# Gate/up products of a hybrid encoder layer: one 512-wide matmul for two 256-wide ones, five PSUM banks per unit, and 21 weight pieces summed during w_out

## The chip, the cores and the metric

One NeuronCore of a Trainium2 chip runs the kernel. The time is device microseconds (us) of one execution. TensorE (PE in the profile) multiplies and accumulates in PSUM, eight banks of 128 x 512 fp32; VectorE (DVE), ScalarE (ACT) and GpSimd (POOL) work beside it, and SyncE (SP) starts most DMAs. Each engine runs its own instructions in order; semaphores tie them together.

## The reference

One encoder layer on 512 tokens of width 2048, all fp32:

```python
h = rmsnorm(x, attn_norm_w)
... # projection w_in, windowed attention, gated linear attention -> concatenated heads
x = x + concat @ w_out
h = rmsnorm(x, ffn_norm_w)
x = x + (silu(h @ w_gate) * (h @ w_up)) @ w_down      # hidden width 5632
return rmsnorm(x, final_norm_w)
```

The change is in h @ w_gate and h @ w_up, each 512 x 2048 times 2048 x 5632.

## The kernel before

**fp32 as two parts.** TensorE takes a rounded fp32 format here. So every operand is split: a rounded part, "hi", cast by ScalarE, and the remainder, "lo" (value minus hi), made by VectorE. A product is three matmuls: hi x hi, hi x lo and lo x hi.

**Buffers.** SBUF work space is two sets of slots, s2 (70 of 128 x 512; "a" in the profile) and s4 (16 of 128 x 1024; "b"). PSUM banks are slots too ("ps"). A slot that is put back goes to the end of its queue of free ones; the next instruction that writes it waits for its last reader.

**Order.** All instructions are written out in one program order. Stages up to w_out are jobs (`run_job`, L268 to L316): each goes through its weights in halves, three matmuls (L304 to L306) per bank and k tile, with weights loaded by SP (512 KB, at most three held) and split up to `AHEAD` = 3 halves ahead. After each half `run_side` takes steps from two lists of generators, `urgent` first. The w_out stage is jobs 12 to 15, one per 512 output columns, 16 halves each; at each job's end VectorE adds the result to x (L1062), POOL loads the next part of x (`load_res`), and `urgent` work squares, stores (xd), transposes and builds the gate/up operands (`pair_operands`, L1028).

**Gate/up (class `Feed`, L1181 to L1283).** Each product of 2 x 2 blocks is done in seven block products instead of eight, at the price of sums before and after (the scheme of Strassen and Winograd). A block of weights is 128 x 128, a block of x is 128 x 256 (half the tokens). There are 44 units: 22 blocks of 256 columns, the gate's and then the up's. A unit goes through the depth of 2048 in 4 pieces; a piece has two pairs of k tiles (p = 0, 1). So there are 176 pieces of 2 x 7 x 3 = 42 matmuls, all 256 wide (L1216 to L1218). Per piece:

- SP loads 512 KB of weights into an s4 slot (L1136), up to three pieces ahead.
- VectorE makes four sums of weight blocks in another slot with three additions (L1157 to L1159), two pieces ahead.
- ScalarE casts three raw blocks (768 columns) and the four sums (1024) to hi (L1170); VectorE makes the remainders (L1175), one piece ahead.
- PE does the products into four banks; two products share a bank.

On the side of x, `pair_operands` makes seven blocks for each pair of k tiles (`xs[q]`, q = 0 to 7): B11, B21, B22 and the sums T1 to T4, each as hi and lo. B11 lies with hi and lo side by side in one slot; the others lie two to a slot, with hi in one slot and lo in another.

After a unit's last piece, `evac` (L1222 to L1246) joins the products in steps, one taken by `run_urgent` in each later piece: ScalarE copies 256 columns out of PSUM (L1232), VectorE adds and subtracts (L1227, the helper's line, and L1235) into an s4 slot. `finish` then scales and applies silu to a gate block (L1253, L1254), or multiplies an up block with the gate's (L1257) and has POOL store it (L1259) for the w_down stage. The first step falls one piece after the unit's end.

`run` (L1262) orders each piece: new banks, loads, split of this piece if still open, sums of the next two, split of the next, products, an urgent step.

Of the kernel before, what the change touches and what calls it, by code (L numbers as in the profile page):

```python
# [23 lines left out]
P = 128  # L24
# [87 lines left out]
def put(*slots):  # L112
    for s in slots:
        if s.home is not None:
            s.home.free.append(s.i)


def layer(nc, tc, x, attn_norm_w, w_in, rel_table, gw_f, gb_f, gw_b, gb_b, gla_norm_w, w_out,
# [7 lines left out]
    with tc.manual_schedule(), \  # L126
# [27 lines left out]
        state = {"credit": 0.0, "set": None}  # L154


        class Stream:
# [93 lines left out]
        class Job:  # L251
            drop = None
            between = None
            tail = None
            banks = None

        def job(kind, pieces, kts, acts, evac, rate=0.0, before=None, start=None, limit=None):

# [9 lines left out]
        def run_job(j):  # L268
# [6 lines left out]
            for i in range(j.n):  # L275
# [754 lines left out]
        def pair_operands(q, fs_):  # L1030

            a, z = slice(0, 256), slice(256, 512)
            f1, f2 = fs_
            t13, t24 = s2.get(), s2.get()
            sub = lambda o, x_, y_: dve.tensor_tensor(o, x_, y_, op=OP.subtract)
            sub(t13.t[:, a], f1.t[:, a], f1.t[:, z])
            sub(t13.t[:, z], f2.t[:, z], f1.t[:, z])
            dve.tensor_tensor(t24.t[:, a], f2.t[:, z], t13.t[:, a], op=OP.add)
            sub(t24.t[:, z], t24.t[:, a], f2.t[:, a])
            yield  # L1040
            todo = []
            slots = []
            for src, n in ((f1.t[:, a], 256), (f2.t, 512), (t13.t, 512), (t24.t, 512)):
                sl, hi, lo, hf = half_split(src, n)
                slots += sl
                todo.append((src, hi, lo, hf))
            for i in range(4):
                src, hi, lo, hf = todo[i]
                act.copy(hi, src)
                sub(lo, src, hf)  # L1050
                put((f1, f2, t13, t24)[i])
                if i % 2:
                    yield
            (_, b1h, b1l, _), (_, f2h, f2l, _), (_, t13h, t13l, _), (_, t24h, t24l, _) = todo
            xs[q] = dict(slots=slots, B11=(b1h, b1l), B21=(f2h[:, a], f2l[:, a]), B22=(f2h[:, z], f2l[:, z]),
                         T1=(t13h[:, a], t13l[:, a]), T3=(t13h[:, z], t13l[:, z]),
                         T2=(t24h[:, a], t24l[:, a]), T4=(t24h[:, z], t24l[:, z]))

        def evac_out(c):
            def f(banks):  # L1060
# [60 lines left out]
        class Blocks:  # L1121
# [9 lines left out]

            def load(self):
                while self.n_load < self.n and len(self.raw) < self.most and s4.free:
                    w, k, n_kt, col, n = self.source(*self.seq[self.n_load])
                    r = s4.get(F32, self.shape(4))
                    sp.dma_start(out=r.t.rearrange("p a b c -> p (a b c)").rearrange("p (k c) -> p k c", k=n_kt),  # L1136
                                 in_=w[k * P:(k + n_kt) * P, col:col + n].rearrange("(k p) c -> p k c", p=P))
                    self.raw[self.n_load] = r
                    self.n_load += 1

            def sums(self, i, halves=False):

# [38 lines left out]
        class Feed(Blocks):  # L1181

            def __init__(self):
                self.units = [(w, j) for j in range(FF // 256) for w in (w_gate, w_up)]
                self.per = NP // 2
                seq = [(u, q) for u in range(len(self.units)) for q in range(self.per)]
                seq.insert(self.per + 1, seq.pop(self.per - 1))  # L1190
                self.begin(seq, 2, P)

            def source(self, u, q):
                w, j = self.units[u]
                return w, 4 * q, 4, j * 256, 256

            def products(self, i, banks):
                st_ = self.sets.pop(i)
                piece = self.seq[i][1]
                first, last = piece == 0, piece == self.per - 1  # L1200
                a, z = slice(0, 256), slice(256, 512)
                A, B, C, E = (b.t for b in banks)
                for p in range(2):
                    q = 2 * piece + p
                    (rh, rl), (sh, sl) = st_
                    R = lambda n: (rh.t[:, p, n], rl.t[:, p, n])
                    Z = lambda n: (sh.t[:, p, n], sl.t[:, p, n])
                    x_ = xs[q]
                    prods = [(A[:, a], R(0), x_["B11"], True), (A[:, z], R(2), x_["B21"], False),
                             (B[:, a], Z(2), x_["T2"], True), (C[:, a], Z(1), x_["T1"], True),  # L1210
                             (C[:, z], Z(0), x_["T3"], False), (E[:, a], Z(3), x_["B22"], True),
                             (E[:, z], R(1), x_["T4"], False)]
                    for o, (wh, wl), (xh, xl), head in prods:
                        head = head and first and p == 0
                        end = last and p == 1
                        mm(o, wh, xh, start=head, stop=False, skip_group_check=True)  # L1216
                        mm(o, wh, xl, start=False, stop=False, skip_group_check=True)  # L1217
                        mm(o, wl, xh, start=False, stop=end, skip_group_check=True)  # L1218
                for hi, lo in st_:
                    put(hi, lo)  # L1220

            def evac(self, u, banks):  # L1222


                a, z = slice(0, 256), slice(256, 512)
                w, j = self.units[u]
                add = lambda o, x_, y_: dve.tensor_tensor(o, x_, y_, op=OP.add)  # L1227
# [4 lines left out]
                act.copy(t1.t[:, a], A[:, a])  # L1232
                add(c[:, a], A[:, z], t1.t[:, a])
                put(banks[0])
                dve.tensor_tensor(t1.t[:, z], t1.t[:, a], B[:, a], op=OP.subtract)  # L1235
                yield
# [7 lines left out]
                put(banks[1])  # L1244
                self.finish(u, c_, c)
                yield  # L1246

            def finish(self, u, c_, c):
                w, j = self.units[u]
                if w is w_gate:  # L1250
                    tables(SILU)
                    for f in range(2):
                        dve.tensor_tensor(c_.t[:, f], c_.t[:, f], rb[2 + f].t, op=OP.mult)  # L1253
                    act.activation(c_.t, c_.t, AF.Silu)  # L1254
                    self.gate = c_
                else:
                    dve.tensor_tensor(c_.t, c_.t, self.gate.t, op=OP.mult)  # L1257
                    put(self.gate)
                    pool.dma_start(out=gd[j], in_=c)  # L1259
                    put(c_)  # L1260

            def run(self):  # L1262
                banks = {}
                for i, (u, q) in enumerate(self.seq):
                    if u not in banks:
                        banks[u] = [ps.get() for _ in range(4)]
                    self.most = 5 if i < 2 else 3
                    self.load()
                    self.split(i)
# [2 lines left out]
                    self.split(i + 1)  # L1272
                    if i < 2:
                        self.sums(self.n_sums, halves=True)
                    self.products(i, banks[u])
                    if u == len(self.units) - 1:
                        for p in (2 * q, 2 * q + 1):
                            put(*xs.pop(p)["slots"])
                        down_start(q)
                    for _ in range(3 if i < 2 else 2 if i < 8 else 1):  # L1280
                        run_urgent()
                    if q == self.per - 1:
                        urgent.append(self.evac(u, banks.pop(u)))  # L1283

        ff = Feed()

# [417 lines left out]
            return run  # L1704

        run_last = finish()
        for n, j in enumerate(jobs):
            if n == n_down:
                dn.run()
# [2 lines left out]
                load_wf()  # L1712
            run_job(j)
            if n == n_out:
                ff.run()
        drain()
        run_last()
# [27 lines left out]
```

## Time and profile before

| | us |
|---|---|
| three runs | 2215.52, 2215.56, 2216.87 |
| median | 2215.56 |
| profiled execution | 2216.53 |
| its span, first to last instruction | 2214.8 |
| w_out stage on PE | about 688 to 863 |
| gate/up stage on PE | 862.8 to 1752.4 |

The profile is of one execution. Its page gives the busy time of each engine, the span in slices, the queues, the chain of work that ended last and the costliest groups of instructions. Further views ask the same trace: groups of a window, waits of one engine with what ended them, instructions in order of time, and tables of windows. The granted TensorE clock was 0.999 of full speed.

### The profile page before, as it was taken

The page shows a single profiled execution, that of the slowest core. Times are in us where ns is not written, and L with a number is a line of the kernel's source. Part 1 is how long each engine was busy: PE and PEld are TensorE (multiplying, and loading weights), DVE is VectorE, ACT ScalarE, POOL GpSimd, SP SyncE. Part 2 cuts the span into 40 slices and gives each one's busy share as a digit, 9 for nine tenths or more (in the row PEclk, how much of TensorE's full clock was granted, in tenths as well). Part 3 has the DMA queues.
Part 4 walks back from the last instruction along what each step waited for, and adds up shares of the span by engine and source line. Part 5 has one row for each costly group of instructions (what it writes and reads, how often), then busy time and mean ns, then how long its engine had stood idle before and what let it go on. Part 6 is the DMA issues. An engine that isn't in the chain of part 4 may idle for free.

```text
span 2214.8 us, 37040 instructions
## 1 busy us (share of the span) xinstructions
PE 2204.3 (100%) x14842; PEld 2040.1 (92%) x14842; DVE 1623.5 (73%) x2740; ACT 1003.0 (45%) x1664; POOL 96.0 (4%) x149
## 2 busy tenths in 40 slices
PE   9999999999999999999999999999999999999998
PEld 7888888888888888999999999999999999999987
DVE  4366665745454438988888888888888888888795
ACT  5244444444444345444434343444343465565462
POOL 0000000000000100000000000000000010011300
PEclk9999999999999999999999999999999999999999
DMA  6525625231324332334334333343333775575982
GB/s 207 162 82 158 169 87 141 76 124 57 96 67 153 131 127 77 115 115 124 115 115 124 115 124 115 115 125 115 115 125 115 249 164 179 167 195 143 288 316 76
DMA packets 210185, 302.26 MB, mean 136 GB/s; under 512 B 15005, under 2 KB 133197, under 8 KB 210014
## 3 DMA queue, kind: packets, MB, share of 16 engines
q1 hardware_dynamic: 194366, 258.87, 37.3%
q0 software_dynamic: 15328, 40.51, 7.2%
q8 instruction: 116, 1.90, 0.4%
q10 hardware_dynamic: 320, 0.53, 0.1%
q14 instruction: 55, 0.45, 0.1%
HBM read 246.58 MB, written 40.70 MB: 130 GB/s over the span
## 4 chain that ended last, share of the span: by engine, by line
PE 99%; DVE 1%; DMA 0%; SPq 0%; ACT 0%; issue 0%; DVEq 0%
PE ps L1217 13%; PE ps L1216 13%; PE ps L1218 13%; PE ps L304 7%; PE ps L306 7%; PE ps L305 7%; PE ps L297 5%; PE ps L295 5%; PE ps L296 5%; PE ps L1457 5%; PE ps L1456 5%; PE ps L1455 5%; PE ps L532 1%; PE ps L872 1%; PE ps L541 1%; PE ps L540 1%
## 5 line engine op out<-in xcount | busy, mean ns | idle before, releaser
L1216 PE MATMUL ps<-a,b 128*128 128x256 f32 x2464 | 697.5, 283 | 0.0
L1217 PE MATMUL ps<-a,b 128*128 128x256 f32 x2464 | 697.3, 283 | 0.0
L1218 PE MATMUL ps<-a,b 128*128 128x256 f32 x2464 | 697.3, 283 | 0.0
L1170 ACT CAST b<-b 128x1024 fp32r<-128x1024 f32 (+1 forms) x473 | 438.7, 941 | 529.1 <-DVE b L1175 280.6
L1175 DVE TENSOR_TENSOR b<-b,b 128x1024 fp32r<-128x1024 f32 (+1 forms) x473 | 501.5, 1087 | 123.3 <-PE ps L1217 61.6
L1217 PEld LDWEIGHTS ps<-a,b 128*128 128x128 f32 x2464 | 473.1, 192 | 0.0
L1216 PEld LDWEIGHTS ps<-a,b 128*128 128x128 f32 x2464 | 473.1, 192 | 0.0
L1218 PEld LDWEIGHTS ps<-a,b 128*128 128x128 f32 x2464 | 473.1, 192 | 0.0
L199 DVE TENSOR_TENSOR a<-b,a 128x512 fp32r<-128x512 f32 x292 | 194.7, 686 | 132.6 <-ACT a L198 121.5
L1456 PE MATMUL ps<-b,a 128*128 128x256 f32 x896 | 253.6, 283 | 0.0
L1457 PE MATMUL ps<-b,a 128*128 128x256 f32 x896 | 253.6, 283 | 0.0
L1455 PE MATMUL ps<-b,a 128*128 128x256 f32 x896 | 253.6, 283 | 0.0
L198 ACT CAST a<-b 128x512 fp32r<-128x512 f32 x292 | 170.8, 618 | 31.9 <-DMA b<-in_w_in_dram 10.9
L304 PE MATMUL ps<-a,a 128*128 128x512 f32 x464 | 182.7, 394 | 0.0
L305 PE MATMUL ps<-a,a 128*128 128x512 f32 x464 | 180.8, 390 | 0.0
L306 PE MATMUL ps<-a,a 128*128 128x512 f32 x464 | 180.7, 390 | 0.0
L1455 PEld LDWEIGHTS ps<-b,a 128*128 128x128 f32 x896 | 172.0, 192 | 0.0
L1456 PEld LDWEIGHTS ps<-b,a 128*128 128x128 f32 x896 | 172.0, 192 | 0.0
L1457 PEld LDWEIGHTS ps<-b,a 128*128 128x128 f32 x896 | 172.0, 192 | 0.0
L1157 DVE TENSOR_TENSOR b<-b 128x512 f32<-128x512 f32 x233 | 159.5, 684 | 10.8 <-DMA b<-in_w_down_dram 10.8
L295 PE MATMUL ps<-a,a 128*128 128x512 f32 x416 | 167.3, 402 | 0.0
L297 PE MATMUL ps<-a,a 128*128 128x512 f32 x416 | 163.0, 392 | 0.1
(240 smaller groups left out, 3059.7 us busy)
## 6 DMA issues: line engine op xcount, KB each, us to landing
b<-in_w_gate_dram SPq DMA_DIRECT2D x88, 512.0 KB, 3.5
b<-in_w_up_dram SPq DMA_DIRECT2D x88, 512.0 KB, 3.9
b<-in_w_down_dram SPq DMA_DIRECT2D x88, 512.0 KB, 4.9
b<-in_w_in_dram SPq DMA_DIRECT2D x48, 512.0 KB, 4.0
b<-in_w_in_dram SPq DMA_DIRECT2D x92, 256.0 KB, 4.4
b<-in_w_out_dram SPq DMA_DIRECT2D x32, 512.0 KB, 5.5
a<-a SPq DMA_DIRECT2D x96, 128.0 KB, 2.3
gd<-b POOLq DMA_DIRECT2D x22, 512.0 KB, 3.2
```

Source lines behind the costliest of these rows:

```text
L295: mm(o, wh.t[:, c], xh.t, start=first, stop=False)
L304: mm(o, xh.t[:, c], wh.t[:, w], start=first and not on, stop=False, skip_group_check=on)
L305: mm(o, xh.t[:, c], wl.t[:, w], start=False, stop=False, skip_group_check=on)
L306: mm(o, xl.t[:, c], wh.t[:, w], start=False, stop=last, skip_group_check=on)
L1170: act.copy(o, src)
L1175: dve.tensor_tensor(o, src, h, op=OP.subtract)
L1216: mm(o, wh, xh, start=head, stop=False, skip_group_check=True)
L1217: mm(o, wh, xl, start=False, stop=False, skip_group_check=True)
L1218: mm(o, wl, xh, start=False, stop=end, skip_group_check=True)
L1455: mm(o, xh[:, t], wh, start=first and h == 0, stop=False, skip_group_check=True)
L1456: mm(o, xh[:, t], wl, start=False, stop=False, skip_group_check=True)
L1457: mm(o, xl[:, t], wh, start=False, stop=last, skip_group_check=True)
```

## The change

1. **Operands of x.** B11, B21, B22, T2 and T4 each get a slot with hi and lo side by side; T1 and T3 stay as they were. Per q ScalarE makes five copies of 256 and one of 512 where it made one and three; the subtractions of VectorE likewise.
2. **Products.** For units after the second (u > 1), three of the seven products (B11, T4, T2) use one 512-wide matmul of the weights' hi with hi and lo of x at once, which leaves hi x hi in the first half of a bank and hi x lo in the second. The two p's follow each other, then the two 256-wide lo x hi go to the first half. A piece has 36 matmuls instead of 42. The loop over the products is now outside that over p, in an order of its own, for all units, and the slots of the three raw blocks are put back after the third product.
3. **Banks and emptying.** Such a unit has five banks, three of them for the wide products, whose halves have to be added. `evac3` does this: three ScalarE copies and five 256-wide VectorE operations in its first step, three operations in the second, then `finish`, split in two steps for a gate block (silu in the second). The first step (of `evac` too, from the second unit on) is emitted right after the unit's last products, before the urgent step. `evac` puts one bank back earlier.
4. **Sums made earlier.** For 21 pieces (the second piece of the gate units u = 2, 4, ... 42), a generator `ahead` runs during jobs 12 to 14, two steps per half: SP loads the weights, VectorE makes the four sums in place by four additions of 256 columns, and POOL stores the slot (512 KB) to a DRAM tile `sd`. In gate/up SP loads it back into an s4 slot three pieces ahead, where VectorE would have made the sums. The piece's raw weights are still loaded and cast as before.

The core of the diff:

```diff
+                state["ahead"] += j.ahead
+                while state["ahead"] >= 1:
+                    state["ahead"] -= 1
+                    next(state["sums"], None)
...
+            for n, (name, f, h) in enumerate((("B11", f1, a), ("B21", f2, a), ("B22", f2, z), ("T2", t24, a),
+                                              ("T4", t24, z))):
+                o = s2.get(F32R, [P, 2, 256])
+                slots.append(o)
+                act.copy(o.t[:, 0], f.t[:, h])
+                sub(o.t[:, 1], f.t[:, h], o.f[:, 0])
+                x_[name] = o.t
...
+            PRODUCTS = (("R", 0, "B11"), ("R", 2, "B21"), ("R", 1, "T4"), ("Z", 2, "T2"), ("Z", 3, "B22"),
+                        ("Z", 1, "T1"), ("Z", 0, "T3"))
+            NARROW = ((0, 0), (0, 1), (3, 1), (1, 0), (3, 0), (2, 0), (2, 1))
+            WIDE = ((0, 0), (1, 0), (2, 0), (3, 0), (1, 1), (4, 0), (4, 1))
...
+            def ahead(self):
+                todo, held = deque(self.pre), deque()
+                def load():
+                    if todo and len(held) < 2 and len(s4.free) > 1:
+                        r = s4.get(F32, self.shape(4))
+                        self.read(todo[0], r)
+                        held.append((todo.popleft(), r))
...
+                    b = lambda n: r.t[:, :, n]
+                    for o, x_ in ((1, 0), (0, 2), (2, 1), (3, 2)):
+                        dve.tensor_tensor(b(o), b(o), b(x_), op=OP.add)
+                        yield
+                    pool.dma_start(out=self.sd[self.pre[i]], in_=r.t.rearrange("p a b c -> p (a b c)"))
+                    put(r)
...
+                    S = s4.get(F32, self.shape(4))
+                    self.S[i] = [S]
+                    sp.dma_start(out=S.t.rearrange("p a b c -> p (a b c)"), in_=self.sd[self.pre[i]])
...
+                        if u > 1 and n in (0, 2, 3):
+                            o = banks[n].t
+                            mm(o, wh, x_.rearrange("p s t -> p (s t)"), start=first and p == 0, stop=False,
+                               skip_group_check=True)
+                            end.append((o[:, 0:256], wl, xh))
...
+                    for p, (o, wl, xh) in enumerate(end):
+                        mm(o, wl, xh, start=False, stop=last and p == 1, skip_group_check=True)
+                    if n == 2:
+                        put(rh, rl)
...
+                m1, m, t4, t2, n = (b.t for b in banks)
+                t, v = s2.get(), s2.get()
+                act.copy(t.t[:, a], m1[:, a])
+                act.copy(c[:, 512:768], t4[:, a])
+                act.copy(c[:, 256:512], m[:, z])
+                add(t.t[:, a], t.t[:, a], m1[:, z])
+                add(c[:, a], m[:, a], t.t[:, a])
+                add(c[:, 512:768], c[:, 512:768], t4[:, z])
+                sub(t.t[:, z], t.t[:, a], t2[:, a])
+                sub(t.t[:, z], t.t[:, z], t2[:, z])
+                put(*banks[0:4])
+                yield
+                add(v.t.rearrange("p (h t) -> p h t", h=2), n.rearrange("p (h t) -> p h t", h=2),
+                    t.t[:, None, z].to_broadcast([P, 2, 256]))
+                add(c[:, 768:1024], n[:, a], v.t[:, z])
+                put(banks[4])
+                add(c[:, 256:768], c[:, 256:768], v.t)
...
+                        banks[u] = [ps.get() for _ in range(5 if u > 1 else 4)]
...
+                    if i + 3 in self.pre:
+                        self.sums(i + 3)
...
+                    if q == self.per - 1:
+                        done = (self.evac3 if u > 1 else self.evac)(u, banks.pop(u))
+                        if u:
+                            next(done)
...
+        for n, j in enumerate(jobs):
+            j.ahead = 2.0 if 12 <= n < n_out else 0.0
```

More of the change, by code (lines that the diff above doesn't have):

```diff
@@ L1200, in products @@
                 first, last = piece == 0, piece == self.per - 1
-                a, z = slice(0, 256), slice(256, 512)
[L1202 to L1218, printed above, removed]
@@ L1219, in products @@
-                for hi, lo in st_:
-                    put(hi, lo)
+                (rh, rl), (sh, sl) = self.sets.pop(i)
+                order = (1, 0, 2, 3) if i in self.pre else (0, 1, 2, 3)
+                open_ = set()
+                for n, (kind, b, x) in enumerate(self.PRODUCTS):
+                    end = []
+                    for p in range(2):
+                        x_ = xs[2 * piece + p][x]
+                        xh, xl = x_ if n > 4 else (x_[:, 0], x_[:, 1])
+                        wh, wl = (rh.t[:, p, b], rl.t[:, p, b]) if kind == "R" else \
+                            (sh.t[:, p, order[b]], sl.t[:, p, order[b]])
+                        if u > 1 and n in (0, 2, 3):
[3 more added lines that the diff above has]
+                            end.append((o[:, 0:256], wl, xh))
+                        else:
+                            bank, half = (self.WIDE if u > 1 else self.NARROW)[n]
+                            o = banks[bank].t[:, half * 256:(half + 1) * 256]
+                            head = first and bank not in open_
+                            open_.add(bank)
+                            mm(o, wh, xh, start=head, stop=False, skip_group_check=True)
+                            mm(o, wh, xl, start=False, stop=False, skip_group_check=True)
+                            mm(o, wl, xh, start=False, stop=last and p == 1, skip_group_check=True)
+                    for p, (o, wl, xh) in enumerate(end):
+                        mm(o, wl, xh, start=False, stop=last and p == 1, skip_group_check=True)
+                    if n == 2:
+                        put(rh, rl)
@@ L1235, in evac @@
                 dve.tensor_tensor(t1.t[:, z], t1.t[:, a], B[:, a], op=OP.subtract)
+                put(banks[1])
                 yield
@@ L1243, in evac @@
                 yield
-                put(banks[1])
-                self.finish(u, c_, c)
+                yield from self.finish(u, c_, c)
                 yield
@@ L1714, in layer @@
             if n == n_out:
+                assert next(state["sums"], None) is None
                 ff.run()
```

81 lines of the change are left out of this document (53 added, 28 removed).

## The prediction

> **What bounds the kernel now.** I read the page first (busy times, chain), then the groups of instructions and the waits of the stage that is changed, then its timeline. The page:
>
> ```profile
> span 2214.8 us, 37040 instructions
> PE 2204.3 (100%) x14842; PEld 2040.1 (92%) x14842; DVE 1623.5 (73%) x2740; ACT 1003.0 (45%) x1664; POOL 96.0 (4%) x149
> PE 99%; DVE 1%; DMA 0%; SPq 0%; ACT 0%; issue 0%; DVEq 0%
> ```
>
> TensorE (PE) is busy for the whole span and the chain that ended last is PE for 99%. All waits of PE in the whole trace, then the gate/up stage by stretches (columns: length, then busy time and instructions of PE, PEld, DVE, ACT, POOL, granted clock, DMA share, GB/s):
>
> ```profile
> PE ps L907 <- DVE warm L388: 1.1, 1, 1.1
> PE ps L346 <- DMA b<-in_x_dram: 0.4, 1, 0.4
> ```
>
> ```profile
> 1000.00:1200.00 200.00, 200.00 (x1669) 200.00 (x1668) 174.68 (x265) 80.95 (x94) 2.67 (x5) 1.00 0.38 118
> 863.00:1753.00 890.00, 890.00 (x7419) 889.91 (x7418) 774.88 (x1184) 372.36 (x452) 12.43 (x24) 1.00 0.38 120
> ```
>
> PE waits 1.5 us in all and never in gate/up, whose 890 us are 40% of the span. So the time here is the number of matmuls times the spacing of their starts, as long as the other engines stay ahead. VectorE (DVE) is the one that might not: 774.9 of 890 us, 87%. ScalarE has 42%.
>
> **The wide matmuls.** The busy figure of one matmul is a pipelined length, so I take starts from PE's timeline (start, length). Inside a piece, and at the two ends of the stage, where it meets 512-wide matmuls:
>
> ```profile
> 1199.83 0.28 PE L1216 MATMUL ps<-a,b 128*128 128x256 f32 x1
> ...
> 1205.95 0.28 PE L1216 MATMUL ps<-a,b 128*128 128x256 f32 x1
> ```
>
> ```profile
> 862.55 0.39 PE L306 MATMUL ps<-a,b 128*128 128x512 f32 x1
> 862.78 0.28 PE L1216 MATMUL ps<-a,b 128*128 128x256 f32 x1
> ```
>
> ```profile
> 1752.31 0.28 PE L1218 MATMUL ps<-a,b 128*128 128x256 f32 x1
> 1752.43 0.40 PE L304 MATMUL ps<-a,a 128*128 128x512 f32 x1
> ...
> 1795.30 0.39 PE L304 MATMUL ps<-a,a 128*128 128x512 f32 x1
> ```
>
> Between the first two rows lie 51 steps: 6.12/51 = 0.1200 us for 256 columns. Between the last two lie 63 triples of L304 to L306: 42.87/189 = 0.2268 us for 512. Twice 256 cost 0.2400, so a pair that becomes one 512 saves 0.0132 us. The mixed order adds nothing that the rows show: 512 followed by 256 takes 0.23, 256 followed by 512 takes 0.12. Count: 42 units (u>1) x 4 pieces x 2 p x 3 products = 1008 pairs, 42 matmuls of a piece becoming 36. 1008 x 0.0132 = **13.3 us** off, a piece going from 5.04 to 4.96 us. In bounds: nothing, if the pair costs 0.24 here, to 13.3; the value taken is the row's own.
>
> The Trainium skill speaks against this ("TensorE: Matmul & The Clock Gate", section "Wait — 56ns, not 53.3ns?"): a fixed 2.5 ns per matmul beyond its columns at 2.4 GHz. By that a pair would save about 2.5 ns (an estimate), 1008 of them 2.5 us. This trace differs: a straight line through its 0.1200 and 0.2268 us leaves 13.2 ns per matmul.
>
> **VectorE in gate/up.** Its groups in this stage (count, busy, mean ns, idle before), then one unit's end in its timeline:
>
> ```profile
> L1175 DVE TENSOR_TENSOR b<-b,b 128x1024 fp32r<-128x1024 f32 x169 | 206.6, 1223 | 7.7 <-PE ps L1217 7.6
> L1175 DVE TENSOR_TENSOR b<-b,b 128x768 fp32r<-128x768 f32 x174 | 166.4, 956 | 91.4 <-PE ps L1217 54.0 <-PE ps L1218 18.7 <-ACT b L1170 16.1
> L1227 DVE TENSOR_TENSOR b<-ps,a 128x256 f32<-128x256 f32 x86 | 36.2, 421 | 1.5
> L1232 ACT COPY a<-ps 128x256 f32<-128x256 f32 x44 | 16.0, 363 | 1.9 <-PE ps L1218 1.9
> ```
>
> ```profile
> 1205.38 0.69 DVE L1157 TENSOR_TENSOR b<-b 128x512 f32<-128x512 f32 x1
> ...
> 1206.90 0.95 DVE L1175 TENSOR_TENSOR b<-b,b 128x768 fp32r<-128x768 f32 x1
> 1208.26 1.23 DVE L1175 TENSOR_TENSOR b<-b,b 128x1024 fp32r<-128x1024 f32 x1 [0.41 <-PE ps L1217]
> 1209.40 0.42 DVE L1227 TENSOR_TENSOR b<-ps,a 128x256 f32<-128x256 f32 x1
> 1209.73 0.41 DVE L1235 TENSOR_TENSOR a<-a,ps 128x256 f32<-128x256 f32 x1
> 1210.06 0.69 DVE L1157 TENSOR_TENSOR b<-b 128x512 f32<-128x512 f32 x1
> ...
> 1213.30 2.10 DVE L1175 TENSOR_TENSOR b<-b,b 128x768 fp32r<-128x768 f32 x2 [1.63 <-PE ps L1217]
> 1215.31 0.69 DVE L1227 TENSOR_TENSOR a<-ps,a 128x512 f32<-128x512 f32 x1
> 1216.03 1.02 DVE L1227 TENSOR_TENSOR b<-ps,a 128x256 f32<-128x256 f32 x2
> 1216.97 0.68 DVE L1157 TENSOR_TENSOR b<-b 128x512 f32<-128x512 f32 x1
> ```
>
> Start to start, a piece's sums take 1.52 us (1205.38 to 1206.90), its split 2.01, the emptying of a unit 0.66 in its first step (1209.40 to 1210.06) and 1.66 in its second. The waits in brackets are for PE to leave the operand buffers: VectorE stands at the end of its lead, it is not late.
>
> The new emptying has five 256-wide operations in its first step, between 0.33 (as the two above) and 0.42 each (421 ns, if each waits for the one before, and three of them do): 1.93 taken. The second step is the same three operations, 1.66. So +1.27 us x 42 = +53 us. The 21 pieces summed earlier take 21 x 1.52 = 32 us away. Net +21 us of VectorE in a stage with 890 - 774.9 = 115 us idle, which gets 13.3 shorter: 81 us, 9%, are left. ScalarE gets two more copies of 0.363 us per unit, 30 us on 42%. So neither is the bound on average, and the cost is put at nothing; the cover is the buffer lead. One place needs care. The unit's emptying now is issued before the next urgent step, and its second add wants a copy of m's second half, which the fifth of seven products fills, 3 x 0.694 + 2 x 0.72 = 3.5 us into the last piece. VectorE is held there for 1 to 2.5 us once per unit, with the next piece's split behind it. Above, the split begun at 1213.30 ended at 1215.40, 2.8 us before PE starts that piece:
>
> ```profile
> 1218.19 0.28 PE L1216 MATMUL ps<-a,b 128*128 128x256 f32 x1
> ```
>
> Of that lead some 0.5 us is left in the worst place, where its 1024 remainder ends that much ahead and its 768 one 1.14 more; PE reads them first 2.5 and 0.45 us into the piece. About 2 us of margin: no stall. Five banks of eight leave three for the next unit; its fourth and fifth (2.1 and 3.5 us into its first piece) are the old m1 and m, which the first two adds and the copies read near the old unit's end; I estimate over 3 us of margin for both. Bounds of the whole: 0 to +1 us per unit (42 us), as VectorE is held up to 2.5 us and the lead was 2.8; 0 taken, by that margin. The reload of ready sums, like any load of these columns, lands about 3.5 us after its issue (first row) and is issued three pieces (15 us) ahead:
>
> ```profile
> b<-in_w_gate_dram SPq DMA_DIRECT2D x88, 512.0 KB, 3.5
> gd<-b POOLq DMA_DIRECT2D x22, 512.0 KB, 3.2
> ```
>
> The operand build (five copies of 256 where there was one of 256 and two of 512) adds 0.2 to 0.3 us of VectorE per q, eight times. It lies in the w_out stage and in the first pieces of gate/up, where VectorE is full:
>
> ```profile
> 872.00:897.00 25.00, 25.00 (x211) 25.00 (x211) 24.24 (x46) 15.75 (x28) 0.00 (x0) 1.00 0.15 44
> ```
>
> Its lead there is built up under full load, so 8 x 0.3 = 2.4 us at most, nothing at least; +0.3 taken, since those in w_out lie beside an idle VectorE. At the hand-over to w_down the emptying's first step (1.93 us for 0.66) stands ahead of the down weights' preparation: 0 to 1.3 us; +0.5 taken.
>
> **The w_out stage.** Jobs 12 to 14 receive 84 adds, 21 x 0.524 = 11.0 MB of loads and as much of stores. At two steps per half this takes 42.5 halves of 12 matmuls of 0.2268, 116 us, with transposes between them (an estimate of 5) 121 us. Rows of that stage, and its DVE group at the jobs' ends:
>
> ```profile
> 732.00:776.00 44.00, 44.00 (x204) 36.60 (x203) 19.70 (x36) 17.54 (x36) 4.31 (x8) 1.00 0.40 137
> 776.00:820.00 44.00, 44.00 (x204) 36.58 (x203) 19.69 (x36) 17.79 (x36) 4.32 (x8) 1.00 0.41 135
> ```
>
> ```profile
> L1062 DVE TENSOR_TENSOR a<-a,ps 128x512 f32<-128x512 f32 x16 | 10.9, 688 | 61.5 <-PE ps L306 61.5
> ```
>
> VectorE: 84 x 0.42 = 35 us over 121 us, 45% rising to about 75%. It now idles waiting for PE at the jobs' ends (61.5 us over four jobs), and the weights are converted three halves (8 us) ahead. Behind a late load of the new pieces the conversions wait; behind the new stores, which wait for their adds, POOL's x loads for the jobs' ends. DMA: 137 GB/s x 121 us = 16.6 MB plus 22.0 = 38.6 MB, or 319 GB/s. Whether the queues give that, other stretches show:
>
> ```profile
> 1752.43:1795.30 42.87, 42.87 (x192) 35.48 (x191) 34.75 (x68) 26.69 (x48) 11.32 (x14) 1.00 0.90 234
> 2090.00:2100.00 10.00, 10.00 (x86) 10.00 (x85) 9.83 (x15) 6.72 (x10) 7.29 (x9) 1.00 1.09 294
> 2120.00:2130.00 10.00, 10.00 (x46) 8.29 (x45) 9.28 (x16) 9.87 (x23) 0.10 (x1) 1.00 1.05 390
> ```
>
> Full queues moved 294 to 390 GB/s; this stage's own mix, 137 at a share of 0.40, would give 342. So it is nearly full but fits, and a load that comes 1 or 2 us late holds VectorE, not PE, thanks to the 8 us lead. 0 to 11 us (38.6 MB at 294 GB/s take 131 us instead of 121) from these rows; +0.5 taken, nearest to the stage's own rate.
>
> **Sum.** -13.3 + 0.3 + 0.5 + 0.5 = -12.0. The profiled execution took 2216.53 (span 2214.8), so 2204.5; the median shown is 0.97 lower, 2215.56: **2203.5**. Own range 2201 to 2206.
>
> **Rivals.**
> A. The emptying makes VectorE late once per unit. For: its 9% of idle time, the in-order hold of up to 2.5 us. Against: 2 us of margin. Each 0.2 us beyond the margin costs 8.4 us over 42 units: 2212, no difference.
> B (other side). The w_out stage becomes bound by DMA. It decides from 38.6/(121+12) = 290 GB/s downwards. The row with 234 GB/s at a share of 0.90 would give 260 when full: 38.6/0.260 = 148 us, 27 more than 121, so 2203.5 + 27 = 2230, slower. For: narrow rows of 1 KB from w_gate, stores and loads mixed. Against: 294 to 390 in full stretches.
> C. The wide pair saves little, 2 to 3 ns of its 240, as the fixed cost would be hidden among narrow matmuls: 1008 x 0.0025 = 2.5, so 2203.5 + 13.3 - 2.5 = 2214, no difference. Against: the spacing at the borders above. This is the skill's rule named there.
> D. Late loads in w_out or late operands at the stage's start cost 3 to 6 us: 2207 to 2209, still faster.
>
> **How the numbers follow.** Forecast 0.76, D 0.08, A 0.05, B 0.07, C 0.04. A measurement of this kernel tells 0.2% (4.4 us) from no change. Faster: forecast and D, 0.84; same: A and C, 0.09; slower: B, 0.07. The range leaves out A, B and C: 2200.5 (no extra cost at all is 2202.3, and the runs scatter by 1.4) to 2209.5.
>
> **What would show it.** Right: starts 0.227 apart behind a wide matmul and 0.120 behind a narrow one; a piece of 36 in 4.96 us; no PE waits in gate/up; VectorE near 91% there, its waits still on PE; PE at 100% in w_out with some 300 GB/s. Wrong: PE waiting for VectorE's remainders after a unit's last piece (A), PE idle in w_out behind a DMA (B), or wide starts 0.237 apart (C).

## The result and the profile after

The changed kernel takes 2202.99 us (median of 4 runs, 2202.5 to 2203.82) where the kernel before takes 2215.55 (4 runs): a ratio of 0.9942, 95% interval 0.9925 to 0.9959, 12.6 us less. The profiled execution took 2202.52, span 2200.8.

The page of the changed kernel, then all waits of PE in its trace:

```profile
span 2200.8 us, 35477 instructions
PE 2189.1 (99%) x13834; PEld 1980.3 (90%) x13834; DVE 1664.8 (76%) x2903; ACT 1029.6 (47%) x1764; POOL 107.2 (5%) x170
```

```profile
PE ps L912 <- DVE warm L393: 1.1, 1, 1.1
PE ps L296 <- ACT a L198: 0.8, 1, 0.8
PE ps L351 <- DMA b<-in_x_dram: 0.4, 1, 0.4
```

1008 matmuls are gone, and PE waits for nothing in w_out, in gate/up or between the stages, as before. The first and the last start of gate/up on PE's timeline (L1274 and L305 are what L1216 and L304 were):

```profile
861.66 0.28 PE L1274 MATMUL ps<-a,b 128*128 128x256 f32 x1
...
1737.98 0.40 PE L305 MATMUL ps<-a,a 128*128 128x512 f32 x1
```

The stage takes 876.32 us; before it was 1752.43 - 862.78 = 889.65. That is **13.33 us less**, and all that the change did: 168 pieces take 0.08 less each, 13.44 in all, and the fourth piece of the stage takes 0.11 more. Up to the stage the changed kernel is 1.12 us ahead (862.78 - 861.66), and that difference is there by 9.6 us, before anything that was changed: the first matmuls, spaced 0.21 us in one execution and 0.11 in the other, reached full spacing at different times. The runs of both kernels scatter by that much. After the stage both traces take 453.20 us to the last matmul.

A piece of gate/up on PE's timeline, from one wide pair at its start to the next piece's:

```profile
1207.26 0.63 PE L1266 MATMUL ps<-a,b 128*128 128x512 f32 x2
1207.73 0.39 PE L1278 MATMUL ps<-a,b 128*128 128x256 f32 x2
1207.96 0.28 PE L1274 MATMUL ps<-a,b 128*128 128x256 f32 x1
...
1212.22 0.40 PE L1266 MATMUL ps<-a,b 128*128 128x512 f32 x1
```

36 matmuls in 4.96 us, and all 168 such pieces take that. But look inside: two wide ones take 0.47 us, 0.235 each and not 0.2268, and the two narrow ones behind them 0.23, 0.115 each and not 0.1200. The two differences nearly cancel.

VectorE at the end of the unit that the prediction showed (L1286 and L1287 are the new emptying, L1167 to L1169 the sums, L1185 the split), then its waits from 1000 to 1700 us and the stretches of the stage:

```profile
1198.67 2.18 DVE L1185 TENSOR_TENSOR b<-b,b 128x768 fp32r<-128x768 f32 x2 [0.61 <-ACT b L1180]
1200.77 0.41 DVE L1286 TENSOR_TENSOR a<-a,ps 128x256 f32<-128x256 f32 x1
1201.46 0.43 DVE L1286 TENSOR_TENSOR b<-ps,a 128x256 f32<-128x256 f32 x1 [0.28 <-ACT b L1294]
...
1202.92 0.69 DVE L1167 TENSOR_TENSOR b<-b 128x512 f32<-128x512 f32 x1
...
1206.45 0.68 DVE L1286 TENSOR_TENSOR a<-ps,a 128x512 f32<-128x512 f32 x1
...
1208.11 0.68 DVE L1167 TENSOR_TENSOR b<-b 128x512 f32<-128x512 f32 x1
...
1209.63 2.09 DVE L1185 TENSOR_TENSOR b<-b,b 128x768 fp32r<-128x768 f32 x2
```

```profile
DVE b L1286 <- ACT b L1294: 34.7, 21, 2.2
DVE b L1185 <- ACT b L1180: 23.6, 36, 1.3
```

```profile
1000.00:1200.00 200.00, 200.00 (x1452) 189.16 (x1451) 179.98 (x282) 89.62 (x119) 2.67 (x5) 1.00 0.41 133
862.00:1738.00 876.00, 876.00 (x6408) 831.12 (x6407) 783.32 (x1247) 394.48 (x535) 12.31 (x24) 1.00 0.41 133
```

The first step takes 1.87 us and the 0.28 of waiting (1200.77 to 1202.92), the second 1.66. VectorE no longer waits for PE to leave the operand buffers, as before, but for ScalarE: for the copy of m's second half (21 times, up to 2.2 us) and for casts. Its lead has shrunk: the split that ends at 1211.72 is for the piece that PE starts at 1212.22, 0.5 us ahead instead of 2.8. It is busy for 89% of the stage.

Why those casts come late matters below. When an up block is finished, POOL stores it (L1350 in this kernel, L1352 in some below) and puts its slot back, and the second `split` after that takes the slot for its 768-column cast (L1180). ScalarE's and POOL's rows ahead of the unit's end above:

```profile
1193.53 0.53 POOL L1350 DMA_DIRECT2D gd<-b  x1 [39.14 <-DVE b L1348]
...
1197.81 1.79 ACT L1180 CAST b<-b 128x768 fp32r<-128x768 f32 x2 [4.11 <-DVE b L1168]
```

The trace names a sum of VectorE (L1168) as the releaser. But this store lands 4.2 us after its issue, at 1197.74, and the cast begins 0.07 us later. So it is for 21 of the 22 stores in every kernel of this case, the one before included (one in e9 has 0.35 us); the last store has no such cast behind it. The cast for the first piece of an up unit thus waits for a store, which lands 4.7 us after its issue on the median, where it took 3.2 before the change. The prediction did not have this chain.

The w_out stage, its first three jobs nearly (the columns as before), VectorE's waits in it, and the DMA issues there:

```profile
687.00:731.00 44.00, 44.00 (x196) 36.45 (x195) 29.56 (x62) 13.38 (x28) 8.57 (x16) 1.00 0.83 279
731.00:775.00 44.00, 44.00 (x204) 36.61 (x203) 30.27 (x70) 18.23 (x40) 7.77 (x15) 1.00 0.90 298
775.00:819.00 44.00, 44.00 (x204) 36.60 (x203) 27.14 (x60) 18.35 (x40) 7.79 (x15) 1.00 0.93 322
```

```profile
DVE b L1237 <- DMA b<-in_w_gate_dram: 17.0, 5, 7.4
```

```profile
b<-in_w_out_dram SPq DMA_DIRECT2D x25, 512.0 KB, 6.5
b<-in_w_gate_dram SPq DMA_DIRECT2D x21, 512.0 KB, 7.8
```

The queues move 279 to 322 GB/s where they moved 128 to 137, loads of w_gate take 7.8 us where the prediction's row had 3.5, and VectorE stands 17 us for them, once for 7.4. PE is at 44.00 of 44.00 in each.

### The profile page after: what moved, and what is told of

The parts are those of the page before. It is cut to its first block, busy times and chain, and to the rows that moved or that the text cites. A ratio compares the mean times of both kernels' runs of the same rounds, so it can differ in the third digit from the quotient of the medians.

```text
span 2200.8 us, 35477 instructions
## 1 busy us (share of the span) xinstructions
PE 2189.1 (99%) x13834; PEld 1980.3 (90%) x13834; DVE 1664.8 (76%) x2903; ACT 1029.6 (47%) x1764; POOL 107.2 (5%) x170
## 4 chain that ended last, share of the span: by engine, by line
PE 99%; DVE 1%; SPq 0%; DMA 0%; ACT 0%; issue 0%; DVEq 0%
PE ps L1266 11%; PE ps L1275 8%; PE ps L1276 8%; PE ps L1274 8%; PE ps L305 7%; PE ps L306 7%; PE ps L307 7%; PE ps L298 5%; PE ps L296 5%; PE ps L1278 5%; PE ps L297 5%; PE ps L1555 5%; PE ps L1554 5%; PE ps L1553 5%; PE ps L537 1%; PE ps L877 1%
## 5 line engine op out<-in xcount | busy, mean ns | idle before, releaser
L1180 ACT CAST b<-b 128x1024 fp32r<-128x1024 f32 (+1 forms) x473 | 433.0, 942 | 541.4 <-DVE b L1185 350.2
L1185 DVE TENSOR_TENSOR b<-b,b 128x1024 fp32r<-128x1024 f32 (+1 forms) x473 | 497.9, 1085 | 57.3 <-ACT b L1180 49.9
L1276 PE MATMUL ps<-a,b 128*128 128x256 f32 x1456 | 411.6, 283 | 0.0
L1275 PE MATMUL ps<-a,b 128*128 128x256 f32 x1456 | 411.4, 283 | 0.0
L1274 PE MATMUL ps<-a,b 128*128 128x256 f32 x1456 | 411.3, 282 | 0.0
L1266 PE MATMUL ps<-a,b 128*128 128x512 f32 x1008 | 317.0, 396 | 0.0
L199 DVE TENSOR_TENSOR a<-b,a 128x512 fp32r<-128x512 f32 x292 | 196.1, 686 | 126.6 <-ACT a L198 115.7
L1275 PEld LDWEIGHTS ps<-a,b 128*128 128x128 f32 x1456 | 278.1, 191 | 0.0
L1276 PEld LDWEIGHTS ps<-a,b 128*128 128x128 f32 x1456 | 278.1, 191 | 0.1
L1274 PEld LDWEIGHTS ps<-a,b 128*128 128x128 f32 x1456 | 277.5, 191 | 0.0
L1278 PEld LDWEIGHTS ps<-a,b 128*128 128x128 f32 x1008 | 189.3, 188 | 44.8
L1278 PE MATMUL ps<-a,b 128*128 128x256 f32 x1008 | 197.5, 277 | 0.0
L305 PE MATMUL ps<-a,a 128*128 128x512 f32 x464 | 182.7, 394 | 0.0
L306 PE MATMUL ps<-a,a 128*128 128x512 f32 x464 | 180.8, 390 | 0.0
L307 PE MATMUL ps<-a,a 128*128 128x512 f32 x464 | 180.7, 389 | 0.0
```

What stands on the lines that cost most here:

```text
L305: mm(o, xh.t[:, c], wh.t[:, w], start=first and not on, stop=False, skip_group_check=on)
L306: mm(o, xh.t[:, c], wl.t[:, w], start=False, stop=False, skip_group_check=on)
L1180: act.copy(o, src)
L1185: dve.tensor_tensor(o, src, h, op=OP.subtract)
L1266: mm(o, wh, x_.rearrange("p s t -> p (s t)"), start=first and p == 0, stop=False, skip_group_check=True)
L1276: mm(o, wl, xh, start=False, stop=last and p == 1, skip_group_check=True)
```

## The experiments

Theory: the time is the matmuls' spacing, and all else is covered. The rivals were those of the prediction: VectorE late in gate/up (A), DMA in w_out (B), wide matmuls that save less (C), late loads or operands (D). Each experiment starts from the changed kernel. Ratios are to the kernel before.

**e1: the sums back in gate/up**, nothing ahead.

```diff
-                    i for i, (u, q) in enumerate(seq) if u > 1 and q == 1 and u % 2 == 0)}
+                    i for i, (u, q) in enumerate(seq) if False)}
...
-            j.ahead = 2.0 if 12 <= n < n_out else 0.0
+            j.ahead = 0.0 if 12 <= n < n_out else 0.0
```

> The 21 pieces' sums go back into gate/up (nothing is loaded, summed or stored ahead in w_out); the wide products and five banks stay. Theory (the time is the matmuls' spacing alone, VectorE has room): VectorE gets 21 x 1.52 = 32 us more in gate/up, 783 of 876 us becoming about 815 (93%), each such piece is made 1.5 us later, the margin of some 2 us holds, and the time stays at 2203 within 1 us. Rival (the earlier sums are what makes the wide products possible): VectorE gets late once per pair of units, 0.5 to 1.5 us each, 2213 to 2235, with PE waiting for the remainders.

2202.80 us, 0.994 (0.9927 to 0.9952): the same as the changed kernel. The stretch of gate/up:

```profile
862.00:1738.00 876.00, 876.00 (x6406) 831.10 (x6405) 811.69 (x1309) 393.90 (x536) 12.83 (x24) 1.00 0.39 121
```

VectorE's 28 us more lie beside PE at 100%, at 93% busy. So the fourth part of the change, with all its traffic, gains nothing in this kernel, and the margin was real.

**e2: narrow matmuls in the five banks.** The halves of the wide ones as two of 256.

```diff
-                            mm(o, wh, x_.rearrange("p s t -> p (s t)"), start=first and p == 0, stop=False,
-                               skip_group_check=True)
+                            mm(o[:, 0:256], wh, xh, start=first and p == 0, stop=False, skip_group_check=True)
+                            mm(o[:, 256:512], wh, xl, start=False, stop=False, skip_group_check=True)
```

> Each wide matmul becomes two 256-wide ones, into the two halves of the same bank; operands, banks, emptying and the earlier sums stay as in the changed kernel. 42 matmuls per piece again. Theory: all of the gain is the 1008 pairs, what surrounds them costs nothing, so the time is that of the kernel before, 2215.5 within 1 us. Rival: the surroundings give or take something that the gain hides: 2214 or less, or 2217 and more.

2216.69 us, 1.0001 (0.9992 to 1.001); pieces of 5.04 us and no wait of PE in the stage. The operands, five banks, emptying and sums ahead together cost nothing and give nothing. The gain is the wide matmul. What in it gives the gain is open: with the width, e2 also puts back the number of matmuls and of weight loads (PEld). Those stood back to back before (889.91 us busy of 890) and no longer do (831.12 of 876), and no run here has narrow matmuls with fewer loads.

**e5: wide, narrow, wide, narrow** instead of two wide ones in a row.

```diff
-                            end.append((o[:, 0:256], wl, xh))
+                            mm(o[:, 0:256], wl, xh, start=False, stop=last and p == 1, skip_group_check=True)
```

> Each wide matmul is followed at once by its own narrow one (wide, narrow, wide, narrow) instead of two wide ones in a row; nothing else. Theory (a matmul's spacing hangs on its own columns, not on its neighbours): 36 matmuls in 4.96 us per piece as before, 2203 within 1 us. Rival (two in a row is needed, a change of width costs a few ns each): 672 more changes of width at 2 to 5 ns make 1.3 to 3.4 us, 2204 to 2206.

2207.06 us, 0.9957 (0.9942 to 0.9972): 4.1 more than the changed kernel, no PE wait in the stage, and nearly every piece takes 4.987 us. The theory that a spacing hangs on its own matmul alone fell; the rival's direction was right. PE's timeline of this kernel (L1268 is the narrow one behind a wide one):

```profile
1200.36 0.39 PE L1266 MATMUL ps<-a,b 128*128 128x512 f32 x1
1200.60 0.28 PE L1268 MATMUL ps<-a,b 128*128 128x256 f32 x1
...
1201.65 0.28 PE L1268 MATMUL ps<-a,b 128*128 128x256 f32 x1
1201.77 0.28 PE L1274 MATMUL ps<-a,b 128*128 128x256 f32 x1
```

Four such couples take 1.41 us, 0.3525 each; in the changed kernel two couples take 0.70 (1207.26 to 1207.96), 0.350 each, and the mean over the stage is 0.3485.

**e10: six wide ones in a row**, then their six narrow ones, as the next guess was that each change of width costs some ns.

```diff
+                end = []
+                for n in ((0, 2, 3, 1, 4, 5, 6) if u > 1 else range(7)):
...
+                    if u > 1 and n == 3:
+                        for k, (o, wl, xh) in enumerate(end):
+                            mm(o, wl, xh, start=False, stop=last and k % 2 == 1, skip_group_check=True)
```

> The changed kernel with all six wide matmuls of a piece in a row, then their six narrow ones, then the narrow products. In e5 six more changes of width in each direction... three more of each kind, cost 0.027 us per piece (4.987 for 4.960), 4.4 ns for each of the six. Theory (each change of width costs some ns beyond the matmul's own spacing): two of three groups less, four changes less, save 4 x 4.4 = 18 ns per piece, 3.0 us over 168: 2200 within 1. Rival (4.960 is the floor that the two spacings give, 6 x 0.2268 + 30 x 0.1200 = 4.961, and only a lone wide matmul costs more): 2203 within 1.

2206.22 us, 0.9956 (0.9943 to 0.9968), pieces of 4.980 us: slower, with fewer changes of width. That guess fell too. Of the three orders, two in a row is the best; what sets the spacing of mixed widths was not found.

**e4 and e9: the sums ahead at four and at three steps per half**, to find where rival B begins.

```diff
-            j.ahead = 2.0 if 12 <= n < n_out else 0.0
+            j.ahead = 4.0 if 12 <= n < n_out else 0.0
```

> The 21 pieces are summed ahead at four steps per half of w_out instead of two, in 60 us instead of 121. The DMA queues are then asked for 22 MB + 137 GB/s x 60 us = 30 MB in 60 us, 503 GB/s, more than the 390 that any stretch of the trace showed. Theory (rival B's mechanism, past its threshold): 30 MB at 320 to 390 GB/s take 77 to 94 us, VectorE waits for the loads with the weights' conversions behind it, and after its lead of 8 us PE stands for 9 to 26 us in w_out: 2212 to 2229. Rival: the queue in front of it soaks it up and the time stays at 2203.

> The changed kernel (three wide products) with the 21 pieces summed at three steps per half of w_out instead of two: 22 MB + 137 GB/s x 80 us = 33 MB in 80 us, 412 GB/s asked for. At four steps 503 GB/s were asked for, 347 moved at the most in a job, and PE lost some 21 us. Theory (rival B, just past its threshold): at 347 GB/s 33 MB take 95 us, 15 too many, 8 of them covered by the lead and some by VectorE's slack: PE loses 2 to 8 us, 2205 to 2211. Rival (only VectorE's blocks of four adds at a time were at fault at four steps): 2203.

Four steps: 2224.57 us, 1.0038 (1.0024 to 1.0051). Three steps: 2209.64, 0.9969 (0.9957 to 0.998).

```profile
PE ps L306 <- DVE a L199: 15.2, 6, 5.8
```

```profile
732.00:777.00 45.00, 34.71 (x140) 27.72 (x140) 29.36 (x69) 16.75 (x39) 10.71 (x20) 0.86 0.99 347
```

At four steps PE waits 15.2 us for VectorE's conversions of w_out (L199), which stand behind additions that wait for their loads (25.0 us in 10 waits), with DMA at 0.99 and 347 GB/s; the clock falls after three of the pauses (below). At three, the same wait:

```profile
PE ps L306 <- DVE a L199: 4.8, 6, 2.8
```

Rival B is a real mechanism, and it begins between the 319 GB/s asked for at two steps and the 412 at three.

**e3: five wide products**, six banks per unit, to see what bounds the next step.

```diff
+            WIDE = ((0, 0), (1, 0), (2, 0), (3, 0), (4, 0), (5, 0), (5, 1))
...
+                        if u > 1 and n < 5:
...
+                m1, m, t4, t2, m22, n = (b.t for b in banks)
...
+                act.copy(c[:, 256:512], m22[:, a])
...
+                add(c[:, a], c[:, a], m[:, z])
...
+                add(c[:, 256:512], c[:, 256:512], m22[:, z])
+                put(*banks[0:5])
...
+                        banks[u] = [ps.get() for _ in range(6 if u > 1 else 4)]
```

> Two more of the seven products (B21, B22) are made wide, in six banks per unit; the emptying gets two more VectorE additions of 256 columns (about 0.7 us per unit, 28 us in all). Theory: 672 more pairs at 0.0132 us save 8.9 us, VectorE goes from 89 to about 93%, two free banks are enough as the third is needed 1.4 us into a unit: 2203.0 - 8.9 = 2194.1 within 1.5. Rival: VectorE or the banks become the bound, PE waits at the units' ends: 2203 or more.

2198.79 us, 0.9918 (0.9905 to 0.9932): about half of the 8.9 us. Most pieces take 4.913 us, but the first three of the up units 4.929, 4.986 and 5.015 on the mean, 0.19 us lost in 8 pieces, 4.0 us in all. VectorE in this kernel, its waits from 1000 to 1700 us, and the store's issue to landing in the same stretch:

```profile
1000.00:1200.00 200.00, 200.00 (x1299) 181.00 (x1298) 188.14 (x302) 88.93 (x121) 2.67 (x5) 1.00 0.42 132
```

```profile
DVE b L1185 <- ACT b L1180: 25.7, 36, 2.0
```

```profile
gd<-b POOLq DMA_DIRECT2D x17, 512.0 KB, 4.9
```

94% busy, against 90% in the changed kernel (179.98 of the same 200 us); the remainders for those pieces end up to 1.9 us after PE has begun them. VectorE is late, as in rival A, but not by its own work alone: it stands 25.7 us for casts, and the cast that opens each up unit waits for the store. A fuller VectorE finishes the block later, so the store starts later and the cast comes later. How much of the 4.0 us is VectorE's work and how much the store's 4.9 us was not tested; a kernel whose cast takes another slot would tell.

**e6, e7 and e8: five wide products, with the sums ahead left out (e6), in the up units' second pieces (e7), in the gate units' third pieces (e8).** e6 is e3 with the edit of e1; e7 and e8 are e3 with the first and the second of these lines:

```diff
+                    i for i, (u, q) in enumerate(seq) if u > 1 and q == 1 and u % 2 == 1)}
...
+                    i for i, (u, q) in enumerate(seq) if u > 1 and q == 2 and u % 2 == 0)}
```

> Five products wide in six banks as in e3, and the 21 pieces' sums back in gate/up as in e1. In e3 VectorE waited 25.7 us in 700 us, 1.45 per 8 pieces, and PE lost about 0.2 per 8 pieces. Theory (VectorE is the bound of five wide products at the ends of units): 1.52 us more per 8 pieces takes what was left and PE loses another 0.1 to 1.0 us per 8 pieces, 2 to 21 us: 2201 to 2220. Rival (the loss of e3 came from the banks, not from VectorE's work): as e3, 2198.8 within 1 us.

> Five wide products as in e3, but the 21 pieces summed ahead are the second pieces of the up units (u = 3, 5, ... 43) instead of the gate units. In e3 PE lost its time in the first three pieces of the up units (4.93, 4.99 and 5.03 us for 4.91), where VectorE's remainders were 0.0 to 0.8 us late, while in the gate units they were 1 us early and more. Theory: the relief falls where VectorE is late, the loss of 4.4 us goes: 2194.5 within 1 us. Rival (VectorE has too little room on the whole, wherever the relief lies): 2198 to 2200.

> Five wide products as in e3, the sums made ahead being those of the third pieces of the gate units instead of the second. In e3 PE lost 4.4 us in the first pieces of the up units; in e7, with the ahead sums in the up units, 48 us, where the reload of the sums waited for an s4 slot (behind the multiply of the up block) and the next weights waited behind it in SP's queue. Theory (VectorE's relief should come just ahead of the place where it is late, and the reload at a time when slots are free): one piece later is nearer to that place and the reload falls before the up unit's emptying, so the loss shrinks from 4.4 us to 0 to 2: 2194.5 to 2197. Rival (the slots decide, and any other place is worse): 2200 or more.

e6: 2234.63 us, 1.0083 (1.0068 to 1.0098), 36 more than e3 and more than the theory's 21. With five wide products the sums ahead are needed; with three (e1) they are not. e7: 2246.56, 1.0135 (1.012 to 1.015), the opposite of what the theory said and none of its rival either.

Most of e7's loss needs no reload: e6, which has none, loses its time in the same pieces. The first three of the up units take 5.97, 5.38 and 5.17 us on the mean in e6, and 6.42, 5.41 and 5.18 in e7. Against e3, e6 loses 36 us and e7 48. In e7 the gate units have lost their relief, as in e6, and the relief for the up units falls where VectorE stands for the cast anyway: from 1000 to 1700 us it waits 30.0 us in e6 and 66.2 in e7 for such casts, 17 times in each. The 12 us between e6 and e7 are what is left for the reload's place. The timeline of e7 at one such place, and the store's row of its DMA issues from 1205 to 1216:

```profile
1207.36 1.22 DVE L1350 TENSOR_TENSOR b<-b,b 128x1024 f32<-128x1024 f32 x1
...
1208.64 0.34 SPq L1247 DMA_DIRECT2D b<-sd  x1
1208.87 0.53 POOL L1352 DMA_DIRECT2D gd<-b  x1 [41.25 <-DVE b L1350]
1209.07 0.39 SPq L1148 DMA_DIRECT2D b<-in_w_up_dram  x1
...
1214.98 1.79 ACT L1180 CAST b<-b 128x768 fp32r<-128x768 f32 x2 [5.72 <-issue]
```

```profile
gd<-b POOLq DMA_DIRECT2D x1, 512.0 KB, 6.0
```

Here the reload of the sums (L1247) takes the slot that the multiply of the up block (L1350) gives back; SP waits 2.1 us for that, with the next weights (L1148) behind it. Reload, weights and the store of the block (L1352) then go at once. The store lands 6.0 us after its issue, and the cast (L1180) begins 0.07 us after that; PE's piece takes 6.5 us instead of 4.9. The trace gives ScalarE's wait no releaser. That it is the store is read from these times and from the order in which the kernel hands out slots. It is not the load issued beside it: in the eight places where that load's landing was recorded, it landed only after the cast had begun.

e8 leaves the relief in the gate units, one piece later: 2196.12 us, 0.991 (0.9895 to 0.9925), the lowest median of all, though one run of e3 (2196.47) lies among its runs. Two pieces of the up units still lose 0.02 to 0.03 us each on the mean.

**e11: four wide products** (B21 too), six banks.

```diff
+                        if u > 1 and n < 4:
...
+                act.copy(c[:, 256:512], m22[:, a])
...
+                add(c[:, a], c[:, a], m[:, z])
```

> Four wide products (B21 too), six banks, one VectorE addition of 256 columns more per unit than in the changed kernel (0.33 us). Theory (the loss of five wide products is VectorE's lateness at the ends of the gate units, which sets in between): 336 more pairs at 0.0118 to 0.0132 us save 4.0 to 4.4 us with VectorE just in time: 2198.5 to 2199.5, no more than five give. Rival (the sixth bank, not VectorE, costs the time): 2201 or more.

2200.99 us, 0.9933 (0.9921 to 0.9945): between theory and rival, and for neither's reason. No piece is late; all take 4.947 us, so that the two further pairs of a piece save 0.0067 us each, half of what the rows of single widths gave. The order of widths has changed again, and no sum of single spacings gives this figure.

VectorE's lead is telling here. VectorE does more than in the changed kernel (186.13 us from 1000 to 1200, against 179.98), and yet the 768-column remainder for the third piece of an up unit ends 3.0 us ahead of it on the mean, where it was 1.3 in the changed kernel and 0.2 behind in e3. The store lands 3.2 us after its issue on the median instead of 4.7 and 4.9. So the lead at this place goes with the store's landing, not with VectorE's load alone.

## Why the prediction was right

The forecast was 2203.5 us, measured 2202.99. The two differ by less than the runs of one kernel do (1.3 us).

- **1008 pairs at 0.0132 us, 13.3 us.** The pieces gave 13.44; e2 shows that nothing else did. One statement in this step was wrong: that "the mixed order adds nothing". The sign that followed from it failed as well: wide starts are 0.235 us apart, no nearer to the 0.227 foretold than to rival C's 0.237, and the narrow ones behind them, at 0.115 instead of 0.120, make it good. Spacings taken from runs of one width predict the sum for this order, not for others: e5 4.987, e10 4.980, e11 4.947 where the rows say 4.961, 4.961 and 4.934. That the sum came out to 0.001 us per piece is partly luck.
- **The rule of 2.5 ns per matmul** that the prediction took from the Trainium skill ("TensorE: Matmul & The Clock Gate", section "Wait — 56ns, not 53.3ns?") would have left 2.5 us. The trace does not agree: 13.44. Rival C fell.
- **VectorE in gate/up at no cost.** Right. The first step was taken at 1.93 us and took 1.87 and a wait of 0.28; the second 1.66 as said. The hold for m's second half (1 to 2.5 us) shows as 34.7 us in 21 waits, up to 2.2. VectorE was said to be near 91% busy; it was 89%. Two things were read wrongly. VectorE's waits are not still on PE but on ScalarE. And the worst place is not behind the hold, where 0.5 us of lead is left as said, but in the third pieces of the up units, behind the cast that waits for the store: there the 1024-column remainder ends 0.17 us ahead of the piece on the mean, and in the last unit 0.91 us after its start. PE reads it first 2.5 us into the piece, by the prediction's count, and no wait follows. e1 adds 28 us and costs nothing, so the margin was larger than needed; e3 and e6 show it used up, two wide products later, in a chain that holds the store as well as rival A.
- **Start of the stage +0.3, hand-over +0.5, w_out +0.5.** Together 1.3 us, measured about 0.1: the fourth piece takes 5.15 us instead of 5.04; the part after the stage is 453.20 in both; in w_out PE runs through, so D did not come either. The w_out term was near its threshold in the way that was said: VectorE stood 17 us, and PE did not.
- **Rival B.** The price was put on the capacity: it would decide from 290 GB/s downwards. The queues gave 322 in a stretch of 44 us, and 347 in one of 45 when asked for more; e9 and e4 show the loss as soon as more is asked for than that.

## What to carry to other kernels

When one engine has no waits, what its instructions are, and how they stand beside each other, is the whole time; the rest of a change is only to be kept from becoming visible. Price mixed instruction widths from the very order that will run, or try two or three orders, since spacings of single widths were off by up to 0.03 us per 36 matmuls here. Work moved to an earlier stage is worth something only where its engine is the bound (nothing with three wide products, 36 us with five), and only at a time when that engine does not stand for something else (e7). When an engine waits, look also for a transfer that still reads the buffer it wants to write: the releaser that a trace names can be another, and a store that slows down beside other traffic holds back whoever takes its slot next.

## What the runs showed of the hardware

The spacing of a 512-wide matmul, 0.2268 us among its like (the L304 rows of the prediction), was 0.231 to 0.235 us on the mean of a kernel among 256-wide ones, whose own fell to 0.115 to 0.119 behind it; the piece's time went with the order and not with the number of changes. No run here tells why.

A 512 KB store landed 3.2 us after its issue on the median in the kernel before and in e11, 4.7 in the changed kernel, 5.6 in e6 and 6.2 in e7, where a reload and a weight load were issued within 0.25 us of it.

After three pauses of PE in e4 (2.71, 5.83 and 4.42 us) the matmuls ran at half speed for some 3 us. PE's timeline at the first, and the granted clock (third figure from the end) right after the pause and then:

```profile
730.52 0.59 PE L306 MATMUL ps<-a,b 128*128 128x512 f32 x1 [2.71 <-DVE a L199]
...
733.04 0.63 PE L306 MATMUL ps<-a,b 128*128 128x512 f32 x1
733.47 0.63 PE L307 MATMUL ps<-a,b 128*128 128x512 f32 x1
...
734.27 0.39 PE L306 MATMUL ps<-a,b 128*128 128x512 f32 x1
```

```profile
731.00:734.00 3.00, 3.00 (x9) 2.32 (x8) 2.22 (x5) 0.00 (x0) 0.81 (x2) 0.50 0.94 286
734.00:737.00 3.00, 3.00 (x14) 2.48 (x13) 2.17 (x6) 0.00 (x0) 0.25 (x1) 0.97 1.08 413
```

0.43 us each instead of 0.23: the nine spacings from 730.52 to 734.27 take 3.75 us where nine of 0.2268 are 2.04, so a wait of 2.71 us cost 1.7 more. A pause of that length need not do it: in e9 PE paused for 2.81 us, up to 747.58, and the clock stayed full:

```profile
748.00:751.00 3.00, 2.73 (x13) 1.93 (x12) 2.31 (x6) 2.36 (x6) 0.54 (x1) 1.00 0.89 272
```

What decides is not shown here. A stall of PE can be dearer than it looks.
